# One P·V accumulation per head over all query blocks, and one 128-row product for each head's 1/rms

## The chip, the cores and the metric

The kernel runs on one core of a Trainium2 chip. The metric is the device time of one execution in microseconds (us); the time before is the median of three runs. TensorE (PE) does the matrix products, VectorE (DVE), ScalarE (ACT) and GpSimd (POOL) the elementwise work, SyncE (SP) issues most transfers.

## The reference

One decoder block on 512 positions of width 1024: a gated convolution branch and a differential attention branch run in parallel from the same normalized input, are merged by gates, and a SwiGLU feed-forward part and a last norm follow. The change lies in the attention branch, which is, cut to what matters:

```python
for i in range(seq_len // Q_BLOCK):              # four query blocks of 128
    kv_len = (i + 1) * Q_BLOCK
    s = jnp.einsum("bqhcd,bkhcd->bhcqk", qs, ks) * scale     # 8 heads, 2 maps c
    s = jnp.where(mask, s, neg)
    p = jax.nn.softmax(s, axis=-1)
    a = p[:, :, 0] - lam * p[:, :, 1]
    outs.append(jnp.einsum("bhqk,bkhe->bqhe", a, vs))
...
o = rmsnorm(o, g_subln[l]) * (1.0 - lambda_init)             # per head, over its 128 columns
y_attn = o.reshape(bsz, seq_len, V_WIDTH) @ w_attn_pw[l]
```

Query block i sees key blocks 0 to i, so of the 16 pairs of a key block j and a query block i ten are used.

## The kernel before, in words

Activations stay on the chip, transposed: a tile has 128 features and 512 positions. Each fp32 operand of a product is split into a rounded high part (a cast on ACT) and the rest (a subtraction on DVE or POOL), and each product is done as three: high·high, low·high, high·low. `split` makes the two parts. The weights come through a queue of 128x1024 blocks (`wr`), which ACT and DVE or POOL split (`wh`, `wl`) a few units ahead of their use.

The program is written out by a generator that keeps a clock for each engine from a small cost model. Long runs of projection products (`chunkA`, 48 matmuls of 512 columns per pair of tiles) are the stream that PE works through; the small steps of attention are generators (`softmaxes`, `outputs`, `head_norm`, `conv_norm`) that the model lets in between when it thinks that their inputs are ready. `pump` fills DVE's idle time in the model with taps of the depthwise convolution (rows `cv<-T,vec_sb,cv`). All this happens when the program is made: on the chip every engine works through a fixed list, and waits wherever an input or a buffer isn't ready. All operations are recorded from one helper, so nearly every row of the profile says L142.

For head h, `softmaxes` computes the scores of the four query blocks, two maps each, into PSUM banks of the pool `at`, which has three banks. Map c's score is two products (rows `at<-T,T` and `at<-kz,T`), then a mask-and-maximum on DVE, an exponential on ACT, and `combine` joins the two maps to a probability block of 128 queries by up to 512 keys. It begins with splits of the head's q and k halves (casts of 64x512 on ACT, subtractions of 64x512 on DVE).

`outputs` then turns the blocks: `turn` takes a group of pairs (j, i), transposes each 128x128 block into one bank of `at` (rows `at<-ident,T`), and splits the bank to two `T5` tiles by a cast on ACT and a subtraction on DVE. `pv` multiplies the parts with V: for each key block j of its group three matmuls, over the query columns that the group has. Before, a head has three groups: (0,0) (0,1) (1,1), which goes as soon as two query blocks are there and has its own accumulation; then (0,2) (0,3) (1,2) (1,3) and (2,2) (2,3) (3,3), which share one. That is 18 matmuls of 256 or 128 columns and two copies of 256 columns out of PSUM.

`head_norm` runs after the last head, between the gate projections. It sums each head's squares by small products, takes the power -1/2 on POOL (`oc`), and turns the result into eight rows of 512, split into `rr[0]` and `rr[1]`. For each head a product with a selector (`sel`, eight rows) spreads that head's row over 128 partitions (`rb`): two matmuls with eight rows each. DVE multiplies the head's output by `rb`, and the product is split for the projection `w_attn_pw` that follows. While that projection runs, `conv_norm` norms the convolution's output: four `cv<-dg,ones` products spread its 1/std, then come eight multiplications on DVE, eight Silu on ACT and eight splits, and the projection `w_conv_pw` reads them.

Of the kernel before, what the change touches and what calls it, by code (L numbers as in the profile page):

```python
# [4 lines left out]
T = 512  # L5
D = 1024
P = 128
# [73 lines left out]
class Model:  # L81
# [9 lines left out]
    def need(self, *aps):  # L91
        return max(self.ready.get(a.tensor.name, 0.0) for a in aps)
# [76 lines left out]
def build(nw):  # L169
# [6 lines left out]
    F32, F32R = mybir.dt.float32, mybir.dt.float32r  # L176
    AF, ALU = mybir.ActivationFunctionType, mybir.AluOpType
# [10 lines left out]
    sel_d = nc.dram_tensor("sel", [8, 8 * P], F32, kind="ExternalInput").ap()  # L188
# [3 lines left out]
    V, S, G, PE = (Engine(model, e, n) for e, n in ((nc.vector, "dve"), (nc.scalar, "act"), (nc.gpsimd, "pool"), (nc.tensor, "pe")))  # L192
    need = model.need
    clk = model.clk

    with tile.TileContext(nc) as tc, contextlib.ExitStack() as homes:  # L196
# [3 lines left out]
        with tc.tile_pool(name="cn", bufs=1) as cn, \  # L200
# [5 lines left out]
            def nm(s):  # L206
                uid[0] += 1
                return f"{s}_{uid[0]}"
# [3 lines left out]
            def tl(tag, dt=F32, w=512):  # L212
                t = home[tag].tile([P, 542 if tag == "T2" else w], dt, name=nm(tag), tag=tag, bufs=BUFS[tag])
                model.alloc(tag, BUFS[tag], t)
                live[tag] = live.get(tag, 0) + 1
                return t
# [3 lines left out]
            def drop(tag, n=1):  # L220
                live[tag] -= n
# [6 lines left out]
            def psum(tag):  # L228
                t = pp.tile([P, 512], F32, name=nm(tag), tag=tag, bufs=PBUFS[tag])
                model.alloc(tag, PBUFS[tag], t)  # L230
                return t

            def load(dst, src, eng=None):
                (eng or nc.sync).dma_start(dst, src)  # L234
                model.load(int(np.prod(dst.shape)) * 4, dst.tensor.name)

            f32 = lambda a: a.bitcast(F32)
# [3 lines left out]
            def mm(out, lhsT, rhs, start, stop):  # L241
                PE.matmul(out, lhsT, rhs, start=start, stop=stop)

            tasks, now = [], [0.0]
# [44 lines left out]
            def until_room(tag, n, reserve=0):  # L289
                while live[tag] + n + reserve > BUFS[tag]:  # L290
                    yield now[0] + 0.3
# [14 lines left out]
            def vcol(base, i=0):  # L306
                return vec[:, base + i:base + i + 1]
# [43 lines left out]
            def split(src, tag, w=512):  # L351
                hi = tl(tag, F32R)
                S.copy(hi[:, :w], src)
                lo = tl(tag, F32R)
                V.tensor_tensor(out=lo[:, :w], in0=src, in1=f32(hi)[:, :w], op=ALU.subtract)
                return hi, lo
# [87 lines left out]
            first = []  # L444
# [237 lines left out]
            def outputs(h, vhl):  # L682
                hh = h % 2
                av = probs[h]

                def turn(grp):
                    n = len(grp) * P
                    yield from until_room("T5", 2)
                    tp = psum("at")
                    yield need(tp, *[av[i] for _, i in grp])  # L690
                    for b, (j, i) in enumerate(grp):
                        PE.transpose(tp[:, b * P:(b + 1) * P], av[i][:, j * P:(j + 1) * P], ident)
                    return split(tp[:, :n], "T5", n)

                def pv(o_ps, grp, aT, first, last):
                    ah, al = aT
                    yield need(o_ps, ah, al, *[t for v in vhl for t in v])
                    js = sorted({j for j, _ in grp})
                    for n, (lo_v, part) in enumerate(((0, ah), (1, ah), (0, al))):
                        off = 0  # L700
                        for j in js:
                            nq = sum(1 for jj, _ in grp if jj == j) * P
                            vs = slice((j % 2) * 256 + hh * P, (j % 2) * 256 + hh * P + P)
                            mm(o_ps[:, 256 - nq:256], vhl[j // 2][lo_v][:, vs], part[:, off:off + nq],
                               first and n == 0 and j == js[0], last and n == 2 and j == js[-1])
                            off += nq
                    drop("T5", 2)

                while finished[0] < h - 1 or 1 not in av:
                    yield now[0] + 0.5  # L710
                ors = tl("T3")
                o_raw.append(ors)
                g = [(0, 0), (0, 1), (1, 1)]
                t0 = yield from turn(g)
                drop("T5", 2)
                o_ps = psum("at")
                yield from pv(o_ps, g, t0, True, True)
                S.copy(ors[:, 0:256], o_ps[:, :256])
                while 3 not in av:
                    yield now[0] + 0.5  # L720
                g1, g2 = [(0, 2), (0, 3), (1, 2), (1, 3)], [(2, 2), (2, 3), (3, 3)]
                t1 = yield from turn(g1)
                t2 = yield from turn(g2)
                drop("T5", 2)
                o_ps = psum("at")
                yield from pv(o_ps, g1, t1, True, False)
                yield from pv(o_ps, g2, t2, False, True)
                S.copy(ors[:, 256:512], o_ps[:, :256])
                if hh:
                    drop("T4", 4)  # L730
                finished[0] = h
# [22 lines left out]
            for h in range(NH):  # L754
                if h % 2 == 0:
                    vhl = []
# [34 lines left out]
            def head_norm():  # L791
                while finished[0] < NH - 1:
                    yield now[0] + 1.0

                ssr = psum("at")
                for h in range(8):
                    yield max(need(o_raw[h]), clk["act"])
                    sq = tl("T5")
                    S.activation(sq, o_raw[h], AF.Square)
                    yield need(sq)  # L800
                    sh, sl = split(sq, "T5")
                    yield need(sh, sl)
                    mm(ssr[0:8, :], pick[:, h * 8:(h + 1) * 8], sh, h == 0, False)
                    mm(ssr[0:8, :], pick[:, h * 8:(h + 1) * 8], sl, False, h == 7)
                    drop("T5", 3)
                rows = tl("T5")[0:8, :]
                V.tensor_scalar(out=rows, in0=ssr[0:8, :], scalar1=1.0 / P, scalar2=1e-6, op0=ALU.mult, op1=ALU.add)
                tp = psum("at")
                yield need(rows, tp)
                for t in range(4):  # L810
                    PE.transpose(tp[:, t * 8:(t + 1) * 8], rows[:, t * P:(t + 1) * P], ident[0:8, 0:8])
                V.tensor_scalar(out=oc, in0=tp[:, 0:32], scalar1=1.0, scalar2=None, op0=ALU.mult)
                drop("T5")
                sel = []
                for a in range(2):
                    sraw = tl("T5")[0:8, :]
                    load(sraw, sel_d[:, a * T:(a + 1) * T])
                    sel.append(sraw)
                G.tensor_tensor(out=oc, in0=oc, in1=mhalf, op=ALU.pow)
                gsub = small(1, "gsub", 1)  # L820
                V.tensor_scalar(out=gsub, in0=vcol(C_GSUB), scalar1=1.0 - LAMBDA_INIT, scalar2=None, op0=ALU.mult)
                tp = psum("at")
                yield need(oc, tp, *sel)
                for t in range(4):
                    PE.transpose(tp[0:8, t * P:(t + 1) * P], oc[:, t * 8:(t + 1) * 8], ident)
                rr = [tl("T5", F32R)[0:8, :] for _ in range(2)]
                S.copy(rr[0], tp[0:8, :])
                V.tensor_tensor(out=rr[1], in0=tp[0:8, :], in1=f32(rr[0]), op=ALU.subtract)
                for a in range(2):
                    sl = tl("T5", F32R)[0:8, :]  # L830
                    S.copy(sl, sel[a])
                    sel[a] = sl
                for h in range(8):
                    rb = psum("at")
                    lt = sel[h // 4][:, (h % 4) * P:(h % 4 + 1) * P]
                    yield need(rb, *rr, *sel)
                    mm(rb, lt, rr[0], True, False)
                    mm(rb, lt, rr[1], False, True)
                    yield need(rb)
                    V.scalar_tensor_tensor(out=o_raw[h], in0=o_raw[h], scalar=gsub, in1=rb, op0=ALU.mult, op1=ALU.mult)  # L840
                    on.append(split(o_raw[h], "T5"))
# [160 lines left out]
            for n in range(2):  # L1002
# [23 lines left out]
                last = [(kk, next_unit()) for kk in range(NF // 2 - tail, NF // 2)]  # L1026
# [55 lines left out]
```

## Time and profile before

| | |
|---|---|
| median of 3 runs | 893.31 us (892.73 to 894.01) |
| profiled execution | 892.93 us |
| its span | 891.1 us |
| mean granted TensorE clock | 0.997 of full speed |
| PE busy in the span | 877.3 us (98%) |
| DVE, ACT, POOL busy | 566.6, 370.2, 293.8 us |

The span is the part of the profiled execution that the trace shows; about 1.8 us lie around it. A matmul's busy time includes its passage through a pipeline, so that neighbours overlap: what one costs is the distance from its start to the start of the next.

### The profile page before, as it was taken

Reading aid. Unit: us, or ns where it says so; the run is one execution under the profiler, and the core shown is the slowest. Engines: PE = TensorE matmul, PEld = TensorE weight load, DVE = VectorE, ACT = ScalarE, POOL = GpSimd, SP = SyncE. Lnnn points to the kernel's source line nnn. Section 1 sums busy time; section 2 is a strip of 40 time slices with the busy share of each in tenths; the row PEclk is TensorE's granted clock in tenths of the full one; section 3 lists DMA queues with packets and bytes.
Section 4 is the critical chain, followed back from the end, with each engine's and each line's share of the span. In section 5 each row is a group of like instructions: output and inputs, shape, how many; then the busy total and the mean of one; then the engine's idle time right before and its main releaser. Section 6 shows DMA issues by size and latency. Waiting matters only on the chain.

```text
span 891.1 us, 11319 instructions
## 1 busy us (share of the span) xinstructions
PE 877.3 (98%) x4246; PEld 731.2 (82%) x4246; DVE 566.6 (64%) x955; ACT 370.2 (42%) x624; POOL 293.8 (33%) x370
## 2 busy tenths in 40 slices
PE   9999999999999999999999999999999999999997
PEld 6778989888888887688888888888888888888886
DVE  6699998999999899947765643433344444323323
ACT  7332237666666675435533433322233332221312
POOL 2775586667767457473000010111111111000001
PEclk9999999999999999999999999999999999999999
DMA  7332222222212222132223432222222223422302
GB/s 243 136 114 100 83 84 71 72 71 71 72 64 80 72 72 96 48 116 89 80 95 142 143 118 94 95 95 95 95 95 95 95 95 94 142 95 71 118 25 95
DMA packets 26584, 85.21 MB, mean 96 GB/s; under 512 B 3088, under 2 KB 4368, under 8 KB 26528
## 3 DMA queue, kind: packets, MB, share of 16 engines
q1 hardware_dynamic: 25952, 83.44, 27.3%
q10 hardware_dynamic: 576, 1.05, 0.3%
q8 instruction: 33, 0.54, 0.2%
q14 instruction: 23, 0.19, 0.1%
HBM read 82.38 MB, written 2.10 MB: 95 GB/s over the span
## 4 chain that ended last, share of the span: by engine, by line
PE 88%; DVE 7%; ACT 2%; issue 1%; DMA 1%; SPq 0%; POOL 0%; POOLq 0%; DVEq 0%; ACTq 0%
PE mm L142 55%; PE at L142 28%; DVE T L142 5%; PE cv L142 4%; ACT T L142 1%; DVE cv L142 1%; DVE kz L142 1%; DMA wr<-wall 1%; DMA T<-xT 1%; ACT wh L142 0%; SPq L234 0%; ACT cv L142 0%; POOL T L142 0%; POOLq L196 0%; POOL sm L142 0%
## 5 line engine op out<-in xcount | busy, mean ns | idle before, releaser
L142 PE MATMUL mm<-T,wh 128*128 128x512 f32 x1360 | 426.4, 395 | 1.3 <-DVE T L142 1.3
L142 PEld LDWEIGHTS mm<-T,wh 128*128 128x128 f32 x1360 | 251.2, 188 | 56.0 <-issue 3.4
L142 PE MATMUL mm<-T,wl 128*128 128x512 f32 x680 | 266.1, 391 | 0.0
L142 POOL TENSOR_TENSOR wl<-wr,wh 128x256 fp32r<-128x256 f32 x244 | 187.0, 802 | 125.7 <-ACT wh L142 119.8
L142 ACT CAST wh<-wr 128x1024 fp32r<-128x1024 f32 (+1 forms) x151 | 149.6, 1015 | 81.3 <-PE mm L142 40.9
L142 POOL TENSOR_TENSOR T<-T,T 128x256 f32<-128x256 f32 (+1 forms) x97 | 91.2, 950 | 240.8 <-DVE T L142 227.6
L142 DVE SCALAR_TENSOR_TENSOR cv<-T,vec_sb,cv 128x512 f32<-128x512 f32 x232 | 160.5, 747 | 0.1
L142 PE MATMUL at<-T,wh 128*128 128x512 f32 x496 | 153.2, 390 | 0.0
L142 PEld LDWEIGHTS mm<-T,wl 128*128 128x128 f32 x680 | 128.0, 188 | 28.2 <-DVE wl L142 0.3
L142 DVE TENSOR_TENSOR wl<-wr,wh 128x1024 fp32r<-128x1024 f32 (+1 forms) x91 | 102.5, 1152 | 70.8 <-ACT wh L142 70.4
L142 DVE TENSOR_TENSOR T<-T,T 128x512 fp32r<-128x512 f32 (+2 forms) x108 | 83.0, 770 | 57.2 <-ACT T L142 56.2
L142 ACT CAST T<-T 128x512 fp32r<-128x512 f32 (+2 forms) x112 | 67.6, 618 | 122.9 <-POOL T L142 77.7
L142 PEld LDWEIGHTS at<-T,wh 128*128 128x128 f32 x496 | 92.7, 188 | 19.0
L142 DVE TENSOR_TENSOR T<-mm,T 128x512 f32<-128x512 f32 (+2 forms) x77 | 52.4, 683 | 80.8 <-PE mm L142 74.8
L142 PE MATMUL mm<-wh,T 128*128 128x256 f32 (+1 forms) x432 | 100.9, 316 | 0.0
L142 PE MATMUL at<-T,wl 128*128 128x512 f32 x248 | 96.7, 390 | 0.0
L142 ACT ACTIVATE T<-T 128x512 f32<-128x512 f32 (+1 forms) x66 | 40.5, 622 | 129.9 <-DVE T L142 129.9
L142 ACT ACTIVATE T<-T,sm 128x128 f32<-128x128 f32 (+3 forms) x100 | 55.9, 561 | 68.3 <-DVE sm L142 63.3
L142 PEld LDWEIGHTS mm<-wh,T 128*128 128x128 f32 x432 | 73.2, 190 | 5.5
L142 DVE TENSOR_TENSOR T<-at,T 128x512 f32<-128x512 f32 (+4 forms) x59 | 38.2, 650 | 59.7 <-PE at L142 55.0
L142 PE MATMUL mm<-wl,T 128*128 128x256 f32 (+1 forms) x216 | 68.2, 316 | 0.0
L142 PEld LDWEIGHTS at<-T,wl 128*128 128x128 f32 x248 | 46.5, 188 | 9.8
(92 smaller groups left out, 645.1 us busy)
## 6 DMA issues: line engine op xcount, KB each, us to landing
wr<-wall SPq DMA_DIRECT2D x144, 512.0 KB, 3.2
T<-xT SPq DMA_DIRECT2D x16, 256.0 KB, 4.4
wr<-wall SPq DMA_DIRECT2D x8, 128.0 KB, 4.4
out<-T SPq DMA_DIRECT2D x4, 256.0 KB, 2.0
out<-T ACTq DMA_DIRECT2D x4, 256.0 KB, 2.6
T<-cs SPq DMA_DIRECT2D x2, 256.0 KB, 4.6
T<-gfin SPq DMA_DIRECT2D x2, 256.0 KB, 3.8
T<-mask SPq DMA_DIRECT2D x1, 256.0 KB, 4.8
```

The source lines that it names most:

```text
L142: r = f(*args, **kw)
```

## The change

In `outputs` nothing is turned until all four query blocks are there. Then three turns come back to back, grouped by key block: key block 0 with all four query blocks, key block 1 with the last three, and (2,2) (2,3) (3,3). The six parts are held together. One accumulation in one bank follows: for key block 0 three matmuls of 512 columns, for 1 three of 384, for 2 three of 256, for 3 three of 128: 12 in place of 18, with the same 3840 columns in all, and one copy of 512 columns.

In `head_norm` the selector tiles and the row tile get all 128 rows, zeroed by three memsets on POOL. The rows' high part stands in rows 0 to 7, the low part in rows 32 to 39, and the selector is loaded twice, to the same rows (four transfers in place of two). One 128-row matmul for each head replaces the two with eight rows.

```diff
                 while finished[0] < h - 1 or 1 not in av:
                     yield now[0] + 0.5
+                while 3 not in av:
+                    yield now[0] + 0.5
                 ors = tl("T3")
                 o_raw.append(ors)
-                g = [(0, 0), (0, 1), (1, 1)]
-                t0 = yield from turn(g)
-                drop("T5", 2)
+
+                parts = []
+                for grp in ([(0, i) for i in range(4)], [(1, i) for i in range(1, 4)], [(2, 2), (2, 3), (3, 3)]):
+                    parts.append((yield from turn(grp)))
+                drop("T5", 4)
                 o_ps = psum("at")
-                yield from pv(o_ps, g, t0, True, True)
-                S.copy(ors[:, 0:256], o_ps[:, :256])
-                while 3 not in av:
-                    yield now[0] + 0.5
-                g1, g2 = [(0, 2), (0, 3), (1, 2), (1, 3)], [(2, 2), (2, 3), (3, 3)]
-                t1 = yield from turn(g1)
-                t2 = yield from turn(g2)
-                drop("T5", 2)
-                o_ps = psum("at")
-                yield from pv(o_ps, g1, t1, True, False)
-                yield from pv(o_ps, g2, t2, False, True)
-                S.copy(ors[:, 256:512], o_ps[:, :256])
+                yield need(o_ps, *[t for pt in parts for t in pt], *[t for v in vhl for t in v])
+                for j in range(4):
+                    ah, al = parts[min(j, 2)]
+                    c0, nq = (256, P) if j == 3 else (0, T - j * P)
+                    vs = slice((j % 2) * 256 + hh * P, (j % 2) * 256 + hh * P + P)
+                    vh, vl = vhl[j // 2]
+                    for n, (v, part) in enumerate(((vh, ah), (vl, ah), (vh, al))):
+                        mm(o_ps[:, j * P:], v[:, vs], part[:, c0:c0 + nq], j == 0 and n == 0, j == 3 and n == 2)
+                drop("T5", 6)
+                S.copy(ors, o_ps)
...
                 for a in range(2):
-                    sraw = tl("T5")[0:8, :]
-                    load(sraw, sel_d[:, a * T:(a + 1) * T])
+                    sraw = tl("T5")
+                    G.memset(sraw, 0.0)
+                    for r in (0, 32):
+                        load(sraw[r:r + 8, :], sel_d[:, a * T:(a + 1) * T])
                     sel.append(sraw)
+                rr = tl("T5", F32R)
+                G.memset(f32(rr), 0.0)
                 G.tensor_tensor(out=oc, in0=oc, in1=mhalf, op=ALU.pow)
...
                 for h in range(8):
                     rb = psum("at")
                     lt = sel[h // 4][:, (h % 4) * P:(h % 4 + 1) * P]
-                    yield need(rb, *rr, *sel)
-                    mm(rb, lt, rr[0], True, False)
-                    mm(rb, lt, rr[1], False, True)
+                    yield need(rb, rr, *sel)
+                    mm(rb, lt, rr, True, True)
```

The first place at which instructions move is a head's turns on PE, here those of the fifth head. A bank is a name `at_...`, `ident` marks a transpose, `kz` a score product and `mm_...` the projection around them; `DVE_49` is a wait for a result or a release by DVE. Before:

```order
L142 MATMUL at_2834<-ident,T_505_2659 128x128 [waits DVE_49]
L142 MATMUL at_2834<-ident,T_518_2745 128x128
L142 MATMUL at_2834<-ident,T_505_2659 128x128
L142 MATMUL at_2834<-ident,T_518_2745 128x128
L142 MATMUL at_2858<-T_502_2638,T_500_2636 128x256 [waits DVE_49]
L142 MATMUL at_2858<-kz_162,T_500_2636 128x256
L142 MATMUL at_2875<-ident,T_505_2659 128x128 [waits DVE_49]
L142 MATMUL at_2875<-ident,T_518_2745 128x128 x2
L142 MATMUL mm_2721<-T_111_589,wh_2498 128x512
```

And of the changed program:

```order
L142 MATMUL at_2838<-ident,T_473_2543 128x128 [waits DVE_49]
L142 MATMUL at_2838<-ident,T_480_2558 128x128
L142 MATMUL at_2838<-ident,T_506_2694 128x128
L142 MATMUL at_2838<-ident,T_519_2768 128x128
L142 MATMUL at_2862<-T_503_2674,T_501_2672 128x256 [waits DVE_49]
L142 MATMUL at_2862<-kz_162,T_501_2672 128x256
L142 MATMUL at_2876<-ident,T_480_2558 128x128 [waits DVE_49]
L142 MATMUL at_2876<-ident,T_506_2694 128x128
L142 MATMUL at_2876<-ident,T_519_2768 128x128
L142 MATMUL at_2891<-ident,T_506_2694 128x128 [waits DVE_49]
L142 MATMUL at_2891<-ident,T_519_2768 128x128 x2
L142 MATMUL mm_2801<-T_100_540,wh_2648 128x512
```

Four tiles of `at` now follow one another where three did: the first turn, a score of the next head, the second turn, the third turn. The pool has three banks, so the fourth, at_2891, is the bank of at_2838.

The second place is ACT's list from the sixth head's turns on. T_618 and T_620 are the high parts of the turn of four blocks (banks at_3135 and at_3122); the 64x512 casts split the next head's q and k. Before:

```order
L142 ACTIVATE T_615_3155,sm_3151<-T_615_3155,sm_3156 128x256 [waits DVE_49]
L142 CAST T_618_3164<-at_3135 128x512 [waits PE_49]
L142 ACTIVATE T_621_3173,sm_3151<-T_621_3173,sm_3174 128x256 [waits DVE_49]
L142 CAST T_623_3180<-at_3170 128x384 [waits PE_49]
L142 CAST T_626_3189<-T_590_3039 64x512 [waits Pool_49]
L142 CAST T_628_3191<-T_592_3059 64x512 [waits Pool_49]
```

And of the changed program:

```order
L142 ACTIVATE T_613_3142,sm_3138<-T_613_3142,sm_3143 128x256 [waits DVE_49]
L142 CAST T_616_3147<-T_567_2949 64x512 [waits Pool_49]
L142 CAST T_618_3149<-T_577_3002 64x512 [waits Pool_49]
L142 CAST T_617_3148<-T_567_2949 64x512
L142 CAST T_619_3150<-T_577_3002 64x512
L142 CAST T_618_3149<-T_577_3002 64x512
L142 CAST T_619_3150<-T_577_3002 64x512
L142 CAST T_620_3173<-at_3122 128x512 [waits PE_49]
```

The cast of the first turn now stands behind six casts of 64x512 that stood behind it before. In the seven heads with a successor this is the only one in which they do.

The third place is the same stretch on DVE in the changed program, from the mask-and-maximum of the score ahead of the turns (printed as ISA) to the first turn's subtraction, the row that reads at_3122:

```order
L142 ISA T_613_3142,sm_3143<-at_3139,T_3_100 128x256 [waits PE_49]
L142 ISA sm_3143 128x1
L142 SCALAR_TENSOR_TENSOR cv_2261<-T_134_794,vec_sb,cv_2261 128x512 [waits DVE_49]
L142 SCALAR_TENSOR_TENSOR cv_2105<-T_124_707,vec_sb,cv_2105 128x512 [waits DVE_49]
L142 SCALAR_TENSOR_TENSOR cv_2261<-T_134_794,vec_sb,cv_2261 128x512 [waits DVE_49]
L142 TENSOR_TENSOR T_616_3147<-T_567_2949,T_616_3147 64x512 [waits Activation_49]
L142 SCALAR_TENSOR_TENSOR cv_2105<-T_124_707,vec_sb,cv_2105 128x512 [waits DVE_49]
L142 SCALAR_TENSOR_TENSOR cv_2261<-T_134_794,vec_sb,cv_2261 128x512 [waits DVE_49]
L142 TENSOR_TENSOR kz_161<-T_577_3002,T_618_3149 64x512 [waits Activation_49]
L142 TENSOR_TENSOR T_617_3148<-T_567_2949,T_617_3148 64x512 [waits Activation_49]
L142 TENSOR_TENSOR kz_162<-T_577_3002,T_619_3150 64x512 [waits Activation_49]
L142 TENSOR_TENSOR T_621_3175<-at_3122,T_620_3173 128x512 [waits Activation_49]
```

Five taps of the convolution and four subtractions of 64x512 stand between the score's row and the subtraction; before, there were two taps.

## Rows read from the trace of the kernel before

**Rows 1.** The page: engines' busy time, and the chain that ended last by engine.

```profile
PE 877.3 (98%) x4246; PEld 731.2 (82%) x4246; DVE 566.6 (64%) x955; ACT 370.2 (42%) x624; POOL 293.8 (33%) x370
...
PE 88%; DVE 7%; ACT 2%; issue 1%; DMA 1%; SPq 0%; POOL 0%; POOLq 0%; DVEq 0%; ACTq 0%
```

**Rows 2.** Timeline of PE: a head's P·V products, projection around them. Columns: start, us, engine.

```profile
151.72 0.80 PE L142 MATMUL at<-T,T 128*128 128x256 f32 x6
152.36 0.68 PE L142 MATMUL mm<-T,wh 128*128 128x512 f32 x2
152.87 0.40 PE L142 MATMUL mm<-T,wl 128*128 128x512 f32 x1
...
159.03 0.87 PE L142 MATMUL at<-T,T 128*128 128x256 f32 x6
159.74 0.63 PE L142 MATMUL mm<-T,wh 128*128 128x512 f32 x2
...
160.43 0.61 PE L142 MATMUL mm<-T,wh 128*128 128x512 f32 x2
```

**Rows 3.** Timeline of PE: the products with eight rows in `head_norm`.

```profile
362.13 0.73 PE L142 MATMUL at<-T,T 8*128 8x512 f32 x2
362.79 0.73 PE L142 MATMUL mm<-T,wh 128*128 128x512 f32 x2
...
363.68 0.73 PE L142 MATMUL at<-T,T 8*128 8x512 f32 x2
```

**Rows 4.** Timeline of PE: its own stalls in attention, in brackets.

```profile
182.51 0.98 PE L142 MATMUL at<-T,T 128*128 128x256 f32 x6 [0.95 <-DVE T L142]
...
226.79 0.38 PE L142 MATMUL at<-T,T 128*128 128x256 f32 x1 [0.82 <-ACT T L142]
...
229.05 0.66 PE L142 MATMUL at<-ident,T 128*128 128x128 f32 x4 [0.69 <-DVE sm L142]
```

**Rows 5.** Timeline of PE: the turns of the fifth head.

```profile
254.21 0.60 PE L142 MATMUL at<-ident,T 128*128 128x128 f32 x4
...
254.88 0.49 PE L142 MATMUL at<-ident,T 128*128 128x128 f32 x3
255.13 0.71 PE L142 MATMUL mm<-T,wh 128*128 128x512 f32 x2
```

**Rows 6.** Timeline of DVE: taps, then the subtraction of that head's four-block turn.

```profile
254.44 1.41 DVE L142 SCALAR_TENSOR_TENSOR cv<-T,vec_sb,cv 128x512 f32<-128x512 f32 x2
255.87 0.69 DVE L142 TENSOR_TENSOR T<-at,T 128x512 fp32r<-128x512 f32 x1
```

**Rows 7.** Timeline of ACT: the cast of the same turn.

```profile
255.27 0.56 ACT L142 CAST T<-at 128x512 fp32r<-128x512 f32 x1
```

**Rows 8.** Timeline of ACT: six casts of 64x512.

```profile
218.16 3.59 ACT L142 CAST T<-T 64x512 fp32r<-64x512 f32 x6
```

**Rows 9.** Timeline of DVE: subtraction of 64x512.

```profile
282.65 0.68 DVE L142 TENSOR_TENSOR T<-T,T 64x512 fp32r<-64x512 f32 x1
```

**Rows 10.** Windows: stretch, sum, busy by engine, granted clock, DMA share, GB/s.

```profile
20.00:50.00 30.00, 28.88 (x129) 23.72 (x128) 21.93 (x32) 12.64 (x19) 24.39 (x27) 0.94 0.36 122
50.00:60.00 10.00, 8.87 (x39) 7.01 (x39) 9.85 (x14) 5.24 (x7) 6.95 (x8) 1.00 0.31 107
```

**Rows 11.** By form: POOL's memset of 64x512.

```profile
L142 POOL MEMSET kz<- 64x512 f32 x4 | 2.1, 520 | 0.2
```

**Rows 12.** Timeline of POOL: the power in `head_norm`.

```profile
352.31 5.46 POOL L142 TENSOR_TENSOR oc<-oc,mhalf 128x32 f32<-128x32 f32 x1 [1.03 <-DVE gsub L142]
```

**Rows 13.** Timeline of PE: the transposes that wait for the power.

```profile
358.87 0.60 PE L142 MATMUL at<-ident,oc 128*8 128x128 f32 x4
```

**Rows 14.** Timeline of PE: the `dg` products of the convolution's norm.

```profile
419.18 1.05 PE L142 MATMUL cv<-dg,ones 128*128 128x128 f32 x8
```

**Rows 15.** Timeline of DVE: splits for the convolution's projection.

```profile
428.45 0.69 DVE L142 TENSOR_TENSOR T<-mm,T 128x512 f32<-128x512 f32 x1 [1.16 <-PE mm L142]
...
436.53 1.29 DVE L142 TENSOR_TENSOR T<-T,T 128x512 fp32r<-128x512 f32 x2 [0.76 <-ACT T L142]
```

More of the change, by code (lines that the diff above doesn't have):

```diff
@@ L693, in turn @@
                     return split(tp[:, :n], "T5", n)
[L695 to L706, printed above, removed]
-                    drop("T5", 2)
                 while finished[0] < h - 1 or 1 not in av:
+                    yield now[0] + 0.5
+                while 3 not in av:
                     yield now[0] + 0.5
@@ L712, in outputs @@
                 o_raw.append(ors)
-                g = [(0, 0), (0, 1), (1, 1)]
-                t0 = yield from turn(g)
-                drop("T5", 2)
+                parts = []
+                for grp in ([(0, i) for i in range(4)], [(1, i) for i in range(1, 4)], [(2, 2), (2, 3), (3, 3)]):
+                    parts.append((yield from turn(grp)))
+                drop("T5", 4)
                 o_ps = psum("at")
-                yield from pv(o_ps, g, t0, True, True)
-                S.copy(ors[:, 0:256], o_ps[:, :256])
-                while 3 not in av:
-                    yield now[0] + 0.5
-                g1, g2 = [(0, 2), (0, 3), (1, 2), (1, 3)], [(2, 2), (2, 3), (3, 3)]
-                t1 = yield from turn(g1)
-                t2 = yield from turn(g2)
-                drop("T5", 2)
-                o_ps = psum("at")
-                yield from pv(o_ps, g1, t1, True, False)
-                yield from pv(o_ps, g2, t2, False, True)
-                S.copy(ors[:, 256:512], o_ps[:, :256])
+                yield need(o_ps, *[t for pt in parts for t in pt], *[t for v in vhl for t in v])
[8 more added lines that the diff above has]
+                S.copy(ors, o_ps)
                 if hh:
@@ L825, in head_norm @@
                     PE.transpose(tp[0:8, t * P:(t + 1) * P], oc[:, t * 8:(t + 1) * 8], ident)
-                rr = [tl("T5", F32R)[0:8, :] for _ in range(2)]
-                S.copy(rr[0], tp[0:8, :])
-                V.tensor_tensor(out=rr[1], in0=tp[0:8, :], in1=f32(rr[0]), op=ALU.subtract)
+                S.copy(rr[0:8, :], tp[0:8, :])
+                V.tensor_tensor(out=rr[32:40, :], in0=tp[0:8, :], in1=f32(rr)[0:8, :], op=ALU.subtract)
                 for a in range(2):
-                    sl = tl("T5", F32R)[0:8, :]
+                    sl = tl("T5", F32R)
                     S.copy(sl, sel[a])
```

## The prediction, made before the result was known

> **What bounds the kernel now.** I read the page first. PE is busy for 877.3 of 891.1 us, and 88% of the chain that ended last is PE [rows 1]. So the time is PE's list of instructions plus the few places where that list stands still, and an edit is worth what it takes from PE's starts or adds to PE's waits. The timeline of PE comes next, read from start to start. Projection products of 512 columns come every 0.23 us (159.74 to 160.43 is 0.69 for three), and six P·V products of 256 columns take 0.71, or 0.118 each [rows 2]. Then I read PE's own stalls: in attention there are three larger ones, 0.95, 0.82 and 0.69 us [rows 4]. Last come the two engines that empty a turn's bank, ACT and DVE, around the turns of one head [rows 5 to 7]: that is the place that the change makes denser.
>
> **P·V, 12 matmuls in place of 18.** Before, a group of three pairs (256 and 128 columns) takes 0.64, and the projection pair behind it 0.51 where 0.46 is usual, so 0.69 with its tail; the group of six takes 0.71 [rows 2]. A head has two of the first and one of the second: 2.09. After, three each of 512, 384, 256 and 128 columns: 0.23, 0.174 (halfway between 512 and 256, an estimate), 0.118, and 0.112 for one of 128 (0.69 / 3 − 0.118), together 1.90. That saves 0.19 a head and **1.5 us** for eight. Without the tails it is 1.99 against 1.85, or 1.1: the range is 1.1 to 1.5, and I take the upper end, since the tail is in the rows. The Trainium skill, "TensorE: Matmul & The Clock Gate", section "Back-to-back issue gap", gives an isolated gap of N/2.4 ns plus 2.5 ns at full clock. By it six matmuls fewer at the same 3840 columns would save 6 × 2.5 ns a head, an estimate of 0.1 us in all, and the time would come out 1.4 higher than the sum below; the same section says that narrow products cost more than that in a real stream, and the rows agree (0.112, not 0.056, for 128 columns).
>
> **1/rms, one product in place of two.** From 362.13 to 363.68 a head's pair and three projection products take 1.55; the three cost 0.69, so the pair costs 0.86, of which 0.66 stand before the next start and the rest lengthens the neighbours [rows 3]. One product with all 128 rows is like its neighbours: 0.23. The gain is 0.63 a head, **5.0 us** for eight; 0.43 a head, 3.4, if the lengthening stayed. I take 5.0, because nothing with eight rows is left there. In that stretch PE has no waits that could swallow it.
>
> **The edits around it in `head_norm`.** The three memsets stand ahead of the power on POOL. The nearest memset took 0.52 us for 64x512 [rows 11], so three are 1.6. POOL idles 1.03 ahead of the power [rows 12], the power ends at 357.77 and PE's transposes that need it start at 358.87 [rows 12, 13]. So 0.5 comes later against a spare 1.1: nothing. Without that cover the cost is 1.6 at most. The two extra transfers of the selector go out on SP in the same gap; weights are queued behind them, and they are small. I take 0 for them.
>
> **The wait that the turns add.** This decides. A turn's bank is free when DVE's subtraction has read it, and that waits for ACT's cast. The changed list has four tiles of the three-bank pool in a row: first turn, a score of the next head, second turn, third turn. The third turn must have the first turn's bank, and between the first turn's last transpose and the third's first stand only a score pair and three transposes. All of the projection stands behind the third turn on PE, and with it what DVE, ACT and POOL take from the projection. In the fifth head of the kernel before, the four transposes start at 254.21 and the second turn is issued by 255.13 [rows 5]; there a third would be due. The cast starts at 255.27, after the exponentials [rows 7], DVE has two taps from 254.44, and the subtraction ends at 256.56 [rows 6]. The bank would be free 1.43 us too late. Before, no one asks for it there. The layout is the same in seven heads (the last has no successor's scores in between); for six of them I take 1.43 each, **8.6 us**. Bounds: with nothing ahead of the cast, the four transposes done at 254.65 plus 0.56 and 0.69 give 255.90, a wait of 0.77, 4.6 for six; with one more tap (0.70) 2.13, 12.8 for six.
>
> In the sixth head the cast stands behind six casts of 64x512 and DVE's subtraction behind five taps and four subtractions. On the fifth head's clock: casts from 255.27 for 3.59 [rows 8], then 0.56 and 0.69, ends at 260.1, 5.0 late. DVE from 254.44: 5 × 0.70, 4 × 0.66 [rows 9] and 0.69 end at 261.3, 6.1 late. The later one counts: **6.0 us**, between 5.0 and 6.2.
>
> "Perfetto Trace Analysis" of the Trainium skill, section "Matmuls", says in one sentence that larger matmuls are more efficient, and in another that independent groups should rotate through different PSUM banks so that emptying one overlaps the next. By the first alone the change would gain what the two paragraphs on products say; by the second the turns lose what this paragraph's neighbours price. The rows on the turns bear out the second.
>
> **The clock.** In the stretch 20 to 50 us, where PE is idle for 1.1 us in all, the granted clock is 0.94 of full, a loss of 1.8 us; in 50 to 60 PE is idle as long in sum and the clock stays at 1.00 [rows 10]. So a stall of a little over one us may pass or may not, and a single one of six should not: half speed of the two levels for a while, **1.8 us**, or 0.
>
> **The stalls of before.** Of those 2.5 us [rows 4] the first was P·V waiting for its split, which now has more work ahead of it, and the others were scores and turns whose inputs came late. PE comes later now, so I take them as gone, **2.5 us**, or 0.
>
> **The convolution's norm.** The head's normed outputs now come sooner, and the model moves the `dg` products: in the changed list 21 projection products lie between them and the convolution's projection, before 48. That projection wants one of eight split tiles every six products, 1.38 us. Before, it starts about 431.0 (419.18 + 0.8 + 48 × 0.23 [rows 14, 2]), wants the last at 440.7, and the last split ends at 437.8 [rows 15]: 2.9 to spare. Twenty-seven products less are 6.2 us, so 3.3 are missing; but DVE waited there for PE, 1.16 in one row and less in others [rows 15], which goes away. I take **1.5 us**, from 0 to 3.3.
>
> **The sum.** +8.6 +6.0 +1.8 +1.5 −1.5 −5.0 −2.5 = +8.9. On the profiled execution's 892.93 that is 901.8; the median of the runs stands 0.4 above the profiled one, so 902 us.
>
> **Rivals.**
> - *The saving comes through.* The turns' banks are free in time, or DVE does the subtraction while PE is at the next product. Then 892.93 − 6.5 (P·V and 1/rms) and up to −2.5 gives 884 to 886.4. For it: before, PE's turns wait for DVE too and hardly stall. Against it: this bank was asked for only much later, and in no row is a bank emptied in under 1.25 us (0.56 and 0.69). It decides if the waits of all heads, the clock and the convolution stay under 7.2 together, that is if six heads cost under 0.35 each with the sixth at 5.0. Chance 0.05.
> - *Waits and savings cancel.* Six at 0.77, the sixth head at 5.0, no clock loss, no wait in the convolution: 4.6 + 5.0 − 9.0 = +0.6, 893.5. For it: ACT may be through with the exponentials when the turn comes. Against it: the exponentials stand ahead of the cast in the list, and taps ahead of the subtraction. Chance 0.10.
> - *More than the sum.* One more tap in each of six heads, the whole of the convolution's 3.3, a clock loss twice: 892.93 + 12.8 + 6.2 + 3.6 + 3.3 − 9.0 gives 910. For it: DVE is the engine nearest to full in attention. Against it: all of them together. Chance 0.10.
> - *The sixth head waits less and the clock stays up:* 5.0 and 0 in place of 6.0 and 1.8: 899. This belongs to the forecast's own spread.
> - *The change doesn't do what it says.* The list shows 12 matmuls and one product a head, so no chance is kept for this.
>
> **How the numbers follow.** The forecast, 897 to 907, has 0.75; the three other cases 0.05, 0.10 and 0.10. The runs before lie within 0.15% of one another, so 0.2%, or 1.8 us, is about what can be told from no change: below 891.5 is faster, 891.5 to 895.1 the same. The saving gives 0.05 for faster, the cancelling 0.10 for the same, the rest 0.85 for slower. The range runs from 894.0, near the cancelling case, to 908.0, short of the worst.
>
> **What would show it.** In the profile after, PE's `at<-ident` transposes of the third turn should show an idle time ended by DVE, about 1.4 us in six heads and 6 in another, and PE's chain should name DVE more often. The 1/rms products should stand 0.23 from their neighbours, with no eight-row matmul left but the transposed sums; P·V should show as 512, 384, 256 and 128 columns in 1.9 us. The clock should dip once after the long stall. The first convolution products should stall on DVE for 1 to 2 us. The prediction is wrong if the third turns start without idle time (then 886), or if DVE reaches the subtraction ahead of the taps; it is wrong in size if the sixth head's stall is hidden by scores that came earlier.

## The result, and the profile after

The changed kernel takes 901.65 us (median of 5 runs, 900.18 to 903.60) against 893.31: a ratio of 1.0098, 95% interval 1.0086 to 1.0109. It is slower, by 8.3 us, where 902 was forecast. The profiled execution is the longest of the five, 903.60 us with a span of 901.8, so 10.7 above the profiled one of before.

The page, as in [rows 1]: busy time, and the chain by engine.

```profile
PE 874.3 (97%) x4190; PEld 731.5 (81%) x4190; DVE 564.3 (63%) x955; ACT 370.0 (41%) x616; POOL 298.1 (33%) x373
...
PE 80%; DVE 11%; ACT 4%; issue 2%; DMA 1%; POOL 1%; SPq 0%; POOLq 0%; DVEq 0%; ACTq 0%
```

PE has 3.0 us less to do and the span is 10.7 longer. The chain moved from PE to DVE and ACT: PE now stands still and waits for them. PE's waits name the place (total us, times, longest):

```profile
PE at L142 <- DVE T L142: 15.0, 8, 6.3
PE mm L142 <- DVE T L142: 1.6, 2, 1.2
```

Seven of the eight are the third turns; the eighth, 1.0, is early in the kernel, at 23.6, and before had it too, with 1.1. The largest waits of attention before were the three of [rows 4]. On PE's timeline the seven are these; the first head's three turns in full, then the third turn of the next six heads (`at<-ident`, three transposes):

```profile
155.33 0.60 PE L142 MATMUL at<-ident,T 128*128 128x128 f32 x4
...
156.00 0.49 PE L142 MATMUL at<-ident,T 128*128 128x128 f32 x3
157.76 0.55 PE L142 MATMUL at<-ident,T 128*128 128x128 f32 x3 [1.26 <-DVE T L142]
...
183.87 0.84 PE L142 MATMUL at<-ident,T 128*128 128x128 f32 x3 [1.38 <-DVE T L142]
...
211.82 0.55 PE L142 MATMUL at<-ident,T 128*128 128x128 f32 x3 [1.38 <-DVE T L142]
...
239.04 0.55 PE L142 MATMUL at<-ident,T 128*128 128x128 f32 x3 [1.39 <-DVE T L142]
...
264.75 0.55 PE L142 MATMUL at<-ident,T 128*128 128x128 f32 x3 [0.96 <-DVE T L142]
...
294.59 0.90 PE L142 MATMUL at<-ident,T 128*128 128x128 f32 x3 [6.26 <-DVE T L142]
...
320.82 0.55 PE L142 MATMUL at<-ident,T 128*128 128x128 f32 x3 [1.38 <-DVE T L142]
```

The idle time in brackets leaves out the tail of a matmul in the pipeline. From start to start the first head's wait is 1.76 − 0.25 (three transposes) = 1.51; the other five that are not the sixth head's give 1.62 four times and 1.19, 9.2 us in all for six, and the sixth 6.5. DVE in the first head shows who is late: taps, then a wait for ACT's cast, then the subtraction, which ends at 157.70, just ahead of PE's 157.76. The cast comes late because a weight's cast of 1.04 stands ahead of it on ACT, from 155.47.

```profile
154.62 2.07 DVE L142 SCALAR_TENSOR_TENSOR cv<-T,vec_sb,cv 128x512 f32<-128x512 f32 x3
157.01 0.69 DVE L142 TENSOR_TENSOR T<-at,T 128x512 fp32r<-128x512 f32 x1 [0.32 <-ACT T L142]
```

In the other five heads of this kind no weight's cast is in the way, and two taps stand ahead of the subtraction. The two queues end together there, to within 0.1 us; the second head, ACT and DVE:

```profile
182.52 0.56 ACT L142 CAST T<-at 128x512 fp32r<-128x512 f32 x1
```

```profile
181.66 1.43 DVE L142 SCALAR_TENSOR_TENSOR cv<-T,vec_sb,cv 128x512 f32<-128x512 f32 x2
183.12 0.69 DVE L142 TENSOR_TENSOR T<-at,T 128x512 fp32r<-128x512 f32 x1
```

So by these rows neither fewer taps alone nor an earlier cast alone would have made that wait shorter by more than 0.1; no run tried it.

In the sixth head, ACT first, then DVE:

```profile
288.78 3.55 ACT L142 CAST T<-T 64x512 fp32r<-64x512 f32 x6
292.24 0.57 ACT L142 CAST T<-at 128x512 fp32r<-128x512 f32 x1
```

```profile
287.01 2.06 DVE L142 SCALAR_TENSOR_TENSOR cv<-T,vec_sb,cv 128x512 f32<-128x512 f32 x3
289.42 0.92 DVE L142 TENSOR_TENSOR T<-T,T 64x512 fp32r<-64x512 f32 x1 [0.34 <-ACT T L142]
290.26 1.40 DVE L142 SCALAR_TENSOR_TENSOR cv<-T,vec_sb,cv 128x512 f32<-128x512 f32 x2
...
293.13 0.69 DVE L142 TENSOR_TENSOR kz<-T,T 64x512 fp32r<-64x512 f32 x1
293.85 0.69 DVE L142 TENSOR_TENSOR T<-at,T 128x512 fp32r<-128x512 f32 x1
```

The turn's cast is done at 292.8, but DVE gets to the subtraction only at 293.85, behind five taps and four subtractions: DVE's queue is the later of the two. (These splits belong to the eighth head, two heads on, not to the next one as the section on the change puts it.) What the stalls do to the clock stands in windows (sum, busy by engine, granted clock):

```profile
184.00:188.00 4.00, 4.00 (x22) 4.00 (x23) 3.44 (x9) 1.75 (x5) 3.92 (x6) 0.58 0.00 0
...
290.00:293.00 3.00, 0.00 (x0) 0.00 (x0) 2.94 (x5) 2.77 (x5) 0.93 (x1) 1.00 0.43 143
293.00:295.00 2.00, 0.41 (x2) 0.41 (x3) 1.94 (x6) 0.09 (x1) 0.00 (x0) 0.55 0.23 90
295.00:300.00 5.00, 5.00 (x15) 3.94 (x14) 3.43 (x8) 2.59 (x6) 1.24 (x2) 0.50 0.00 2
```

After the 6 us the clock is at the lower level (1.2 of 2.4 GHz) until 300, 2.5 us lost in the last row; it was lowered in this run behind the second head's two stalls too, 1.7 us. In the stretch 20 to 50 us, where the profiled execution of before lost 1.8 [rows 10], it stayed up, and PE waited 0.7 us longer for a `dg` tile instead. The two all but cancel, as the first head's first `kz` product shows, before and after:

```profile
131.09 0.28 PE L142 MATMUL at<-kz,T 128*128 128x128 f32 x1
```

```profile
130.92 0.28 PE L142 MATMUL at<-kz,T 128*128 128x128 f32 x1
```

The gains are there as well. One head's P·V, the twelve under the name of the first's shape, and what follows:

```profile
345.00 2.02 PE L142 MATMUL at<-T,T 128*128 128x512 f32 x12
346.86 0.68 PE L142 MATMUL mm<-T,wh 128*128 128x512 f32 x2
347.37 0.39 PE L142 MATMUL mm<-T,wl 128*128 128x512 f32 x1
```

That is 1.86, and 0.05 more on the pair behind it (0.51 for 0.46): 1.91 against 2.09 from [rows 2]. And two heads' 1/rms products:

```profile
379.08 0.39 PE L142 MATMUL at<-T,T 128*128 128x512 f32 x1
...
379.99 0.39 PE L142 MATMUL at<-T,T 128*128 128x512 f32 x1
```

0.91 from one head to the next, where [rows 3] give 1.55. Last, the convolution's projection waits once, at 442.25: 0.79 from the start before it where 0.23 is usual.

```profile
441.46 0.39 PE L142 MATMUL mm<-T,wh 128*128 128x512 f32 x1
442.25 0.50 PE L142 MATMUL mm<-T,wh 128*128 128x512 f32 x1 [0.39 <-DVE T L142]
```

### The profile page after: what moved, and what is told of

Its sections match the earlier page's. It is cut to its first block, busy times and chain, and to the rows that moved or that the text cites. A ratio compares the mean times of both kernels' runs of the same rounds, so it can differ in the third digit from the quotient of the medians.

```text
span 901.8 us, 11219 instructions
## 1 busy us (share of the span) xinstructions
PE 874.3 (97%) x4190; PEld 731.5 (81%) x4190; DVE 564.3 (63%) x955; ACT 370.0 (41%) x616; POOL 298.1 (33%) x373
## 4 chain that ended last, share of the span: by engine, by line
PE 80%; DVE 11%; ACT 4%; issue 2%; DMA 1%; POOL 1%; SPq 0%; POOLq 0%; DVEq 0%; ACTq 0%
PE mm L142 50%; PE at L142 26%; DVE T L142 8%; PE cv L142 4%; ACT T L142 3%; DVE cv L142 2%; DVE kz L142 1%; ACT wh L142 1%; DMA wr<-wall 1%; DMA T<-xT 1%; SPq L234 0%; POOL wl L142 0%; DVE sm L142 0%; ACT cv L142 0%; POOL T L142 0%
## 5 line engine op out<-in xcount | busy, mean ns | idle before, releaser
L142 PEld LDWEIGHTS mm<-T,wh 128*128 128x128 f32 x1360 | 254.5, 189 | 56.1 <-DVE T L142 2.9
L142 ACT CAST T<-T 128x512 fp32r<-128x512 f32 (+1 forms) x112 | 67.6, 617 | 119.9 <-POOL T L142 77.7
```

Source lines behind the costliest of these rows:

```text
L142: r = f(*args, **kw)
```

## The experiments

**One part at a time.** `rms_only` is the kernel before with the change's `head_norm`; `pv_only` is the kernel before with the change's `outputs`.

> The kernel before with the 1/rms products alone changed. Theory: eight pairs that cost 0.86 each become eight products of 0.23, 5.0 us less, and the convolution's projection waits about 0.5 us, as in the changed kernel: 888.8 us, faster than before by 0.4 to 0.6%. Rival: the saving is swallowed by later waits or by the memsets ahead of the power: 892 to 894, no difference.

> The kernel before with the P.V part alone changed. Theory: the third turn waits for the first turn's bank in seven heads, about 15 us of waits and 2 to 4 us of clock against 1.5 us of products and 2.5 us of old stalls: 905 to 907 us, slower than the whole change by the 4.5 us that the 1/rms part saves. Rival: the loss comes from the 1/rms part or from both together: under 897.

Measured: `rms_only` 889.93 us (889.60 to 890.30; ratio 0.9963, 0.9948 to 0.9978), 3.2 below the 893.09 of the kernel before, measured beside it; `pv_only` 906.40 us (904.67 to 907.57; 1.0145, 1.0125 to 1.0165), 13.3 above it. So the loss is the P·V part's alone, and the 1/rms part gains, 1.1 less than expected when it stands alone; on top of the P·V part it is worth 4.8 (906.40 to 901.65). The profiled `rms_only` shows two waits that the products' saving ran into, both for the convolution's norm, which now comes sooner:

```profile
401.99 1.13 PE L142 MATMUL cv<-T,ones 128*128 128x512 f32 x2 [0.65 <-DVE T L142]
...
429.46 0.50 PE L142 MATMUL mm<-T,wh 128*128 128x512 f32 x1 [0.39 <-DVE T L142]
```

From start to start they cost 0.8 and 0.55, where about 0.5 in all was expected. `pv_only` has the waits of the changed kernel to a tenth of a us:

```profile
PE at L142 <- DVE T L142: 14.9, 8, 6.3
```

**Is it the bank?** `third_mm` keeps the turns back to back and takes the third turn's bank from the projection's pool. `late_bank` takes a turn's bank when its blocks are there.

```diff
 third_mm
-                    tp = psum("at")
+                    tp = psum("mm" if grp[0][0] == 2 else "at")
                     yield need(tp, *[av[i] for _, i in grp])
 late_bank
-                    tp = psum("at")
-                    yield need(tp, *[av[i] for _, i in grp])
+                    yield need(*[av[i] for _, i in grp])
+                    tp = psum("at")
+                    yield need(tp)
```

The second needs a word on the planner. Its `alloc` notes, when a tile is taken, which older tile of the pool gives up its bank: the oldest taken. In the changed kernel the first turn's tile is taken, then waits for its last block, and the next head's scores take theirs meanwhile. By the planner's list the third turn's tile then replaces one of those scores, long emptied; on the chip it gets the first turn's bank. So the planner sees no wait and puts nothing in between.

> The changed kernel with the third turn's bank from the projection's pool of three, so that the turns stay back to back. Theory: the third turn no longer waits for the first turn's subtraction, and the projection has a spare bank for most of the time: 885 to 891 us. Rival A: the wait only moves, to the projection's next tile, which has to wait for the third turn's split: 893 to 900. Rival B: the bank is not the cause: 901.

> The changed kernel with a turn's bank taken from the pool when its probability blocks are there, not before the wait for them, so that the program's planner knows which bank is given next. In its order three projection products stand ahead of the third turn, and the third turn gets the bank of the score ahead of the first turn. Theory: the waits of 15 us and the clock's loss go almost wholly, 884 to 889 us, faster than before. Rival: DVE is too late in general and the third turn waits anyway for its release: 896 or more.

Measured: `third_mm` 888.85 us (888.57 to 890.62; 0.9956, 0.9941 to 0.9970), `late_bank` 887.20 (886.79 to 888.04; 0.9933, 0.9918 to 0.9948). With the same turns in a row and another bank the third turn follows at once:

```profile
155.02 0.60 PE L142 MATMUL at<-ident,T 128*128 128x128 f32 x4
...
155.70 0.49 PE L142 MATMUL at<-ident,T 128*128 128x128 f32 x3
156.02 0.49 PE L142 MATMUL mm<-ident,T 128*128 128x128 f32 x3
```

So it does in all seven heads, which settles the bank as the cause. The time is 12.8 us below the changed kernel's for one name of a pool; the planner lays out the rest anew after the edit, so this is the bank's price together with what moved. Some waiting is left: PE's waits ended by DVE's mask-and-maximum (`sm`), which empties a score's bank, are 4.8 us in five, where the changed kernel has 0.9 in two. The longest are 1.88 for a score, at 242.35, and 1.72 for the seventh head's first turn, at 298.03. In `late_bank` the planner sees the wait, puts the score pair ahead and three projection products between, and no third turn waits:

```profile
154.84 0.93 PE L142 MATMUL at<-ident,T 128*128 128x128 f32 x7
...
156.30 0.49 PE L142 MATMUL at<-ident,T 128*128 128x128 f32 x3
```

**The sixth head.** `sixth_first` holds the eighth head's splits back until the sixth head's turns are written out.

```diff
                 while started[0] < h - 2:
                     yield now[0] + 0.5
+                while h == 7 and turned[0] < 5:
+                    yield now[0] + 0.3
...
                     parts.append((yield from turn(grp)))
+                turned[0] = h
```

> The changed kernel with the eighth head's q and k splits held back until the sixth head's third turn is written out, so that neither the six casts of 64x512 on ACT nor the four subtractions on DVE stand ahead of the sixth head's first turn; the turns' order on PE stays. Theory: three taps remain ahead of the subtraction, the third turn's wait falls from 6.3 us to about 2.1, and no clock loss follows it there: 895 to 898 us. Rival: the long wait comes from DVE's taps or from the blocks, not from the splits: 5 us or more remain, 900 to 902.

Measured: 895.00 us (894.48 to 896.39). The third turn of that head now waits about as long as the others, with three taps ahead of the subtraction:

```profile
285.21 0.60 PE L142 MATMUL at<-ident,T 128*128 128x128 f32 x4
285.89 0.49 PE L142 MATMUL at<-ident,T 128*128 128x128 f32 x3
288.18 0.55 PE L142 MATMUL at<-ident,T 128*128 128x128 f32 x3 [1.79 <-DVE T L142]
```

6.26 became 1.79, 4.5 us, and the time fell by 6.65. The granted clock of this profile is 1.00 in every window of ten us from 0 to 460, so the clock's loss behind that stall (2.5 us in the changed kernel's profile) fits the other 2.2 us; that it makes up all of them is not shown.

**Is the fused product worth anything once the wait is gone?** `late_all` takes the banks of scores and accumulations late as well; `old_pv_late` is the 18 matmuls of before, in their three groups, with the 1/rms change and late turn banks.

> late_bank, with the banks of the scores and of the P.V accumulation also taken from the pool only when their inputs are there. Theory: what is left of PE's waits in attention in late_bank (some 5 us) comes from late probability blocks and not from the planner's view of the banks, so nothing changes: 886 to 888. Rival: the planner's view causes these too: 883 to 885.

> The kernel before (18 P.V matmuls in three groups) with the 1/rms change and with a turn's bank taken late, as in late_bank. Theory: what the 12 products save in a kernel without bank waits is 1.5 us of PE and some of the old stalls, so this is 1 to 3 us above late_bank: 888 to 890. Rival: the fused product is worth nothing, since its turns stand closer together: 886 to 887.5.

Measured: `late_all` 886.82 (885.30 to 887.55; 0.9915, 0.9894 to 0.9935), `old_pv_late` 886.97 (886.22 to 887.33; 0.9917, 0.9895 to 0.9940). The first is no different from `late_bank`, as expected, but not for the reason expected: its waits moved (the longest on `sm` is 0.8 in place of 1.5, and one of 1.24 for a projection tile is new, at 198.5) and came to the same sum. The second is a miss: without the fused product the kernel is as fast. PE's waits show most of the reason, of `late_bank`:

```profile
PE mm L142 <- DVE T L142: 2.8, 2, 1.5
PE at L142 <- DVE sm L142: 2.6, 3, 1.5
```

and of `old_pv_late`:

```profile
PE mm L142 <- DVE T L142: 1.2, 1, 1.2
...
PE at L142 <- DVE sm L142: 0.6, 2, 0.4
```

The two larger ones of `late_bank` are a score product whose bank DVE empties late, and a projection product that waits for its bank:

```profile
179.75 0.39 PE L142 MATMUL at<-T,T 128*128 128x256 f32 x1 [1.49 <-DVE sm L142]
...
271.84 0.73 PE L142 MATMUL mm<-T,wh 128*128 128x512 f32 x2 [1.54 <-DVE T L142]
```

At both places DVE works without a pause and is behind by 1.5 us. These are waits for banks, not for late probability blocks, as the expectation of `late_all` had it. All of PE's waits together are 9.2 us in `late_bank` and 6.9 in `old_pv_late`; the 2.3 less stand against 1.5 us more in products, and the time moved by 0.2, so about 0.6 stays unexplained.

Three more kernels were measured side by side: `late_bank` again, `late_18` and `old_pv_late_all`. `late_18` has `late_bank`'s turns and cuts the products back to twelve of 256 and six of 128 columns.

```diff
                     for n, (v, part) in enumerate(((vh, ah), (vl, ah), (vh, al))):
-                        mm(o_ps[:, j * P:], v[:, vs], part[:, c0:c0 + nq], j == 0 and n == 0, j == 3 and n == 2)
+                        for c in ((slice(0, 256), slice(256, T)) if j == 0 else (slice(P, 256), slice(256, T)) if j == 1 else (slice(j * P, T),)):
+                            mm(o_ps[:, c], v[:, vs], part[:, c0 + c.start - j * P:c0 + c.stop - j * P],
+                               j == 0 and n == 0 and c.start == 0, j == 3 and n == 2)
```

> late_bank once more, on the chip of the next two, so that they can be compared within one call: 887.2 us.

> late_bank with its turns as they are, but the products cut back to the widths of before: 18 matmuls, twelve of 256 columns and six of 128. Theory: the twelve products do save 0.18 us a head on PE, and what old_pv_late showed (no gain) is because turning all blocks at the end costs as much in waits; then this is 1.0 to 1.8 us above late_bank, 888.2 to 889. Rival: the product's shape is worth nothing even with the same turns: within 0.5 us of late_bank.

> old_pv_late with the banks of the scores and of the P.V accumulation also taken late. Theory: like late_all against late_bank, no change beyond 1 us: 886 to 888, so the fused product has no advantage in any of these orders. Rival: the early first turn gains from it, 885 or less, or loses, over 888.

Measured: 887.46 us (887.02 to 887.77), 888.08 (887.49 to 888.78) and 888.16 (887.13 to 889.67). A head's 18 products take 2.05 in `late_18`:

```profile
305.20 2.21 PE L142 MATMUL at<-T,T 128*128 128x256 f32 x18
307.25 0.67 PE L142 MATMUL mm<-T,wh 128*128 128x512 f32 x2
```

So the shape saves 0.19 a head on PE, 1.5 us in eight, as the sum has it; the time moved by 0.6, which is less than the 1.0 to 1.8 expected, since PE's other waits in `late_18` are a little shorter (about 0.8 in all, against `late_bank_again`). `late_bank` and `late_18` have the same two waits for DVE, 1.49 and 1.54 in the one, 1.49 and 1.28 in the other, so these go with the order and not with the shape; `old_pv_late` has no wait over 0.5 us there and pays the 1.5 us in products. The orders come out within a us or so of each other: `old_pv_late_all`, a little over its 886 to 888, is 0.7 above `late_bank_again`, with ranges that overlap. Why DVE is behind at those two places in the one is not shown.

**What an eight-row product costs.** `rms_twice` does `rms_only`'s product twice.

```diff
                     mm(rb, lt, rr, True, True)
+                    mm(rb, lt, rr, True, True)
```

> rms_only with each head's 128-row product done twice, the first overwritten. Theory: a second product costs 0.23 like any other, so 1.8 us more in all, and of the 0.86 that a pair with eight rows cost 0.40 came from its shape and not from their number: 891.5 to 892. Rival: two products into one bank in a row cost more, as the eight-row pair did: 0.86 a head, 895.

One run: 890.78 us. A pair with 128 rows takes 0.45 and leaves its neighbours alone:

```profile
366.59 0.62 PE L142 MATMUL at<-T,T 128*128 128x512 f32 x2
367.04 0.62 PE L142 MATMUL mm<-T,wh 128*128 128x512 f32 x2
...
367.72 0.62 PE L142 MATMUL at<-T,T 128*128 128x512 f32 x2
```

1.13 from head to head, where two eight-row products gave 1.55 [rows 3]. Of the 0.63 that a head saves, 0.23 is the one product less and 0.40 the shape. That holds for the distances on PE. In the time of this one run, below the 891.5 to 892 expected, only 0.9 of the 1.8 shows; the two waits of `rms_only` at 402 and 429 are not in this profile, nor is one of 0.9 that it has at 8.1.

## Why the prediction was right, point by point

The forecast of 902 for the median and 901.8 for the profiled execution met 901.65 and 903.60. The mechanism was as forecast. That the median was met to 0.4 is in part luck: by the profiled execution, from which the terms were summed, the forecast is 1.8 short, and several terms are off by 0.5 to 1 in either direction. The terms, by that execution:

- *The waits of six heads*, 8.6 forecast at 1.43 each: 9.2, between 1.19 and 1.62. The two taps were there in five heads; in the first there were three, and ACT's cast behind a weight's cast ended the wait. The mechanism, the third turn's bank, was shown by `third_mm` and `late_bank`.
- *The sixth head*, 6.0 forecast from DVE's queue: 6.5, and DVE's queue is what ended it. (The sum took 0.66 for a subtraction where [rows 9] show 0.68; in this head they came 0.72 apart.) `sixth_first` took 4.5 us of it away by moving the splits.
- *The clock*, 1.8 forecast, once: 2.5 after the sixth head and 1.7 after the second, less the 1.8 that before lost early on. In `pv_only`'s profile only the first of these occurs. The second may come and go from run to run: the five runs' mean granted clock lies between 0.991 and 0.995, and the run at 0.995 is the fastest, 900.18 us; which of the two losses they had is not shown.
- *The convolution's norm*, 1.5 forecast: 0.55 in the changed kernel, 1.35 in `rms_only` with the mean's product. This term was mis-sized: of the wide bounds, 0 to 3.3, the lower part was right.
- *P·V*, 1.5 forecast: 0.18 a head, 1.45. *1/rms*, 5.0 forecast: 0.64 a head, 5.1.
- *The stalls of before*, 2.5 forecast to go: the three went, and one of 0.47 is new, at 181.26, ahead of the second head's turns; about 2.0. The reason given, late inputs, does not fit the last of the three: by [rows 4] it ended with DVE's `sm`, the mask-and-maximum that empties a score's bank, and so did the new one. So by the trace the kernel before had a bank wait already.

Worked out: 9.2 + 6.5 + 2.4 + 0.55 − 1.45 − 5.1 − 2.0, and 0.7 for the `dg` tile, is 10.8 against the measured 10.7. The agreement is closer than the terms are. The early part stands in this sum as 1.1 saved (1.8 of clock less 0.7 of `dg`), but by the first `kz` product it saved 0.2. With that the terms make 11.7, while PE's last matmul starts 9.96 later (894.26 for 884.30), and 0.7 of the 10.7 lie behind it. So they overstate by 1.7, and the rows don't show which.

What the forecast didn't see is behind the numbers: it took three banks and four tiles for the whole cause, and the wait for unavoidable in that layout. The planner fills it when it knows of it, as `late_bank` shows. And the fused product's own gain, right on PE, is hardly one of the kernel: the order that it needs, all turns at the end, goes along with waits for DVE of the same size.

The best versions are 6 us below before and 14 to 15 below the changed kernel: `late_all` and `old_pv_late`, 886.8 and 887.0, with `late_bank` at 887.2 not told apart from them.

## What to carry to other kernels

Before several tiles of a small pool are put in a row, follow the bank of the last one back to its former owner, and read from the trace when the engines that empty it will be through; what stands ahead in their queues counts as much as the cast and the subtraction themselves (here 0.56 and 0.69 us of waits of 1.2 to 6.5). Where a planner orders the program, a buffer should be taken when it can be used: taken early, the planner's idea of who frees it and the pool's differ, and the wait is planned nowhere. A saving in one engine's products should be measured beside the order that it needs: here another order without it was as fast.

## What the runs showed of the hardware

Two products with eight rows cost 0.86 us with what they add to their neighbours, two with 128 rows and the same 512 columns 0.45. The Trainium skill, "TensorEngine Tiling (Array Packing)", section "Key Properties", says that a change of tiling mode needs a drain. The lengthened neighbours in [rows 3] would fit that; whether a product with eight rows is such a change, no run here shows.

A stall of PE of 1 to 1.4 us may or may not lower the clock: of the six such third turns of the changed kernel one was followed by four us at 0.58 of full clock, the others by none below 1.00, and in `pv_only` no one of the six was. In `third_mm` the stall of 1.88 was followed by four us at 0.57, the one of 1.72 by four at 1.00. The 6.3 us of the sixth head were followed by half clock in both profiles.
